# A two-layer decoder step on Trainium2: VectorE's weight sums tied behind a job's third sum, two PSUM products moved ahead of a square, and the norm's eps moved ahead of a low part

## The chip, the core and the metric

The kernel runs on one core of one Trainium2 chip. The metric is the device time of one execution in microseconds (us), the median of three runs; lower is better. The engines are named as in the profile: PE is TensorE (PEld its weight loads), DVE is VectorE, ACT is ScalarE, POOL is GpSimd, SP is SyncE, whose queue issues most loads.

## The reference, cut to what matters

```python
def rmsnorm(x, g):
    y = xf * lax.rsqrt(jnp.mean(xf * xf, axis=-1, keepdims=True) + RMS_EPS)
    return (y * g).astype(x.dtype)

def swiglu(x, w_gate, w_up, w_down):
    return (jax.nn.silu(x @ w_gate) * (x @ w_up)) @ w_down

def short_conv_mixer(x, buf, w_in, w_conv, w_out):
    b, c, h = jnp.split(x @ w_in, 3, axis=-1)
    u = c * h
    full = jnp.concatenate([buf, u], axis=1)
    y = sum(w_conv[j] * full[:, j:j + L] for j in range(CONV_WIDTH))
    return (b * y) @ w_out, full[:, -(CONV_WIDTH - 1):]

def trunk(...):                          # layer 0: short convolution, layer 1: retention
    for i in range(DEPTH):
        h = rmsnorm(x, norm_mix[i])
        m, st = short_conv_mixer(h, ...) if i % 2 == 0 else retention_mixer(h, ...)
        x = x + m
        x = x + swiglu(rmsnorm(x, norm_ffn[i]), ffn_w_gate[i], ffn_w_up[i], ffn_w_down[i])
    return rmsnorm(x, final_norm), ...
```

The model width is 1024, the FFN's hidden width 2816; 512 prompt tokens and 32 sample tokens are handled together, so a token axis has 544 columns, in two halves of 272 (`HT`). All is float32.

## The kernel before, in words

**Precision.** A float32 product is made of three faster matmuls: each operand is split into a high part (`h`, `wh`, a copy on ACT) and a low part (`l`, `wl`, the difference, on DVE), and high·high, high·low and low·high are summed in PSUM. `split` makes both parts; `mixed` makes the low part's first half on DVE and its second half with an accumulating DMA that POOL issues.

**Jobs.** Most projections are done two 128-row output tiles at a time, as a 2×2 block product in seven instead of eight products (`Job`). `weights7` loads the two weight tiles on SP's queue into three rotating buffers (`w`), and makes four sums of them on DVE (lines 357 to 360 before the change: `s1 = a21 + a22`, `s2 = s1 - a11`, `a21 = a11 - a21`, `w4 = a12 - s2`) and then the parts p1 (products 1 and 2), p2 (6 and 5), p3 (7 and 4) and p4 (3), which are named `wh/wl`, `h2/l2`, `wh/wl` and `h4/l4`. One product is 12 matmuls of 272 columns (line 411). Each product's PSUM result is handed on at once: `u1`, `u2`, `p5` and the last one, `c21`, are copied by ACT, while `c11`, `c12` and `u3` are added by DVE (line 516). The accumulator of products 1, 6, 7, 4 is one PSUM bank: product 4 may not write it before DVE has read it for `u3`, the sum behind product 7. `run` prepares the weights of job i+1 when job i begins.

**Order.** The instructions are recorded in the order of the code, and a scheduler that works with estimated costs then sets the order on each engine; each engine works its queue off in that order. `tc.issue_after(x)` keeps the instructions in its block behind `x` where both are on one engine.

**The convolution.** `start` makes the first output tile of b, c and h directly from x as it arrives, `products` the second one; the norm's scale `R` comes only later, so the results are multiplied by `R` (b) or `R2 = R·R` (c) behind the products (lines 674 to 677). Then come eight jobs (h and b of tiles 2 and 3; c, h and b of tiles 4, 5 and of 6, 7).

**The norms in front of the FFN.** `rms_scale` is a generator whose steps are woven between the matmuls of the first two FFN jobs: five matmuls with the mean's column (line 274), eps on DVE (line 249) and the power on POOL (line 252), some empty steps (`rest`), and five matmuls that spread the result over the partitions (line 256), which ACT copies into `R` (lines 285 and 286). `paced(steps, 4)` leaves out the first four places.

Of the kernel before, what the change touches and what calls it, by code (L numbers as in the profile page):

```python
# [52 lines left out]
def hybrid_decode_kernel(ctx: ExitStack, tc: tile.TileContext, a: dict, o: dict):  # L53
    nc = tc.nc
# [143 lines left out]
    def halves(t):  # L198
        return t.rearrange("p (a b) -> p a b", a=2)
# [57 lines left out]

    def rms_scale(sample=False, pt=None, rest=4):

# [6 lines left out]
        for tt in range(n):  # L266
# [8 lines left out]
            if tt < n - 1:  # L275
                yield
        rsqrt(rN[:, :n], ms[:, :n], n)
        for _ in range(rest):
            yield
# [57 lines left out]

    def weights7(src1, src2, sw, n, adding=False, spare=None, first=1, fourth=False, whole=False, later=()):

# [14 lines left out]
        with ExitStack() as behind:  # L354
            for made in later:
                behind.enter_context(tc.issue_after(made.ins))
            nc.vector.tensor_add(s1, a21, a22)
            nc.vector.tensor_sub(s2, s1, a11)
            nc.vector.tensor_sub(a21, a11, a21)
            nc.vector.tensor_sub(w4, a12, s2)  # L360

        behind, p1, p2 = last_minus[0], parts2(2 * n), parts2(2 * n, sw, ("h2", "l2"))
        if whole:
            split(*p1, w1)
        else:
            (split_adding if adding else mixed)(*p1, w1, src1)
        with tc.issue_after(behind.ins) if adding else ExitStack():
            split(*p2, w2)
        p3 = parts2(2 * n)
        with ExitStack() as after:  # L370
            for made in later:
                after.enter_context(tc.issue_after(made.ins))
            mixed(*p3, w3, src2)
        p4 = parts2(n, sw, ("h4", "l4"))
        with tc.issue_after(behind.ins) if adding else ExitStack():
            split(*p4, w4)

# [109 lines left out]

    def run(jobs, order, after, steps, ahead=False):

        jobs[0].order = order  # L490
        jobs[0].begin()
        jobs[0].weave = jobs[1].weave = steps
        for i, job in enumerate(jobs):
            nxt = jobs[i + 1] if i + 1 < len(jobs) else None
            if nxt is not None:
                nxt.prepare()
            apart = i == 0 and (ahead or not order)
            job.middle(nxt if apart else None)
            if nxt is not None and not (i == 0 and ahead):
                nxt.begin()  # L500
            job.end()
            after(i)

    last_add = [None]

    def summed(dst, finish):


        def take(what, src):
# [3 lines left out]
            if what in first:  # L513
                nc.scalar.activation(first[what], src, AF.Copy)
            elif what in more:
                last_add[0] = nc.vector.tensor_add(more[what], more[what], src)  # L516
            finish(what, src)

# [4 lines left out]
    with ExitStack() as c0:  # L523
# [148 lines left out]
        pts.append(products(1, range(3), steps))  # L672
        signal(0)
        nc.vector.tensor_mul(R2, R, R)
        for d, r, j in ((c, R2, 1), (b, R, 0)):
            nc.vector.tensor_mul(halves(d[:, 0, :]), halves(d[:, 0, :]), r)
            each(lambda p, di, ri: nc.vector.tensor_mul(di, p, ri), pts[1][j], halves(d[:, 1, :]), r)
        for i in range(2):
# [55 lines left out]
        mixed_in(b, taps(0), 0)  # L734
        run(jobs, (2, 5, 6), lambda i: None, iter(()), True)

# [18 lines left out]
    def ffn(layer, next_gain, then=None):  # L755
        with ExitStack() as c1:
# [194 lines left out]
            if layer == 1:  # L951
                jobs[0].places["later"] = [residuals[5]]
            jobs[0].prepare(layer == 1)
            made_in = MADE if layer == 0 else list(range(KT))
# [16 lines left out]

            steps = paced(rms_scale(rest=7), 4)
            run(jobs, (), after, steps)
# [929 lines left out]
```

## Time and profile before

| | |
|---|---|
| median of three runs | 1387.44 us (1385.43 to 1388.99) |
| the profiled execution's own time | 1386.94 us |
| its span | 1385.2 us |
| PE, PEld, DVE, ACT, POOL busy | 99%, 95%, 82%, 59%, 16% |
| HBM | 158 GB/s read and written over the span |

The span is the stretch from the first to the last instruction of the program; 1.7 us of the profiled execution lie around it. PE is busy nearly all the time, so the first question for each edit is whether PE waits at that place. A PE that waits for a semaphore for a short time is hardly seen in busy shares: it is seen in the distance between the starts of neighbouring matmuls.

### The profile page before, as it was taken

The page shows a single profiled execution, that of the slowest core. Times are in us where ns is not written, and L with a number is a line of the kernel's source. Part 1 is how long each engine was busy: PE and PEld are TensorE (multiplying, and loading weights), DVE is VectorE, ACT ScalarE, POOL GpSimd, SP SyncE. Part 2 cuts the span into 40 slices and gives each one's busy share as a digit, 9 for nine tenths or more (in the row PEclk, how much of TensorE's full clock was granted, in tenths as well). Part 3 has the DMA queues.
Part 4 walks back from the last instruction along what each step waited for, and adds up shares of the span by engine and source line. Part 5 has one row for each costly group of instructions (what it writes and reads, how often), then busy time and mean ns, then how long its engine had stood idle before and what let it go on. Part 6 is the DMA issues. An engine that isn't in the chain of part 4 may idle for free.

```text
span 1385.2 us, 26505 instructions
## 1 busy us (share of the span) xinstructions
PE 1375.7 (99%) x10420; PEld 1313.7 (95%) x10420; DVE 1134.0 (82%) x1929; ACT 822.9 (59%) x1288; POOL 217.8 (16%) x249
## 2 busy tenths in 40 slices
PE   9999999999999999999999999999999999999998
PEld 9999999999999999999978887887899999999997
DVE  6988889898989888777868586586799898989875
ACT  7666567667667656767641413224377767667654
POOL 0111011212222213211200000000112212221212
PEclk9999999999999999999999999999999999999999
DMA  6477347777777754777666455475756777777752
GB/s 224 115 162 169 109 107 162 176 169 179 151 184 154 165 126 123 201 175 221 187 230 228 149 186 201 136 261 183 220 131 157 171 176 173 155 178 166 165 111 88
DMA packets 99438, 232.89 MB, mean 168 GB/s; under 512 B 9809, under 2 KB 33889, under 8 KB 98929
## 3 DMA queue, kind: packets, MB, share of 16 engines
q1 hardware_dynamic: 68464, 167.26, 39.2%
q0 software_dynamic: 28400, 55.82, 23.4%
q10 hardware_dynamic: 2448, 8.12, 1.5%
q8 instruction: 81, 1.33, 0.4%
q14 instruction: 45, 0.36, 0.1%
HBM read 191.05 MB, written 28.42 MB: 158 GB/s over the span
## 4 chain that ended last, share of the span: by engine, by line
PE 94%; DVE 3%; ACT 1%; DMA 1%; issue 0%; POOL 0%; DVEq 0%; SPq 0%; POOLq 0%; ACTq 0%
PE sm L411 43%; PE mm L411 16%; PE mm L187 14%; PE sm L187 5%; PE sm L1344 2%; PE sm L1345 2%; PE sm L1346 2%; PE sm L175 2%; PE sm L176 1%; PE sm L177 1%; PE sm L1594 1%; DVE ol L203 1%; DMA w<-in_cvin_dram 1%; PE mm L1355 1%; PE mm L1612 1%; PE mm L1522 1%
## 5 line engine op out<-in xcount | busy, mean ns | idle before, releaser
L411 PE MATMUL sm<-oh,wh 128*128 128x272 f32 x856 | 247.2, 289 | 1.3 <-DVE h L516 1.3
L411 PE MATMUL sm<-ol,wh 128*128 128x272 f32 x856 | 246.2, 288 | 0.0
L411 PE MATMUL sm<-oh,wl 128*128 128x272 f32 x856 | 246.1, 288 | 0.0
L202 ACT ACTIVATE h<-w 128x512 fp32r<-128x512 f32 (+3 forms) x171 | 137.7, 805 | 85.8 <-PE mm L411 77.6
L203 DVE TENSOR_TENSOR l<-w,h 128x512 fp32r<-128x512 f32 (+3 forms) x171 | 154.6, 905 | 23.2 <-ACT h L202 21.0
L333 ACT ACTIVATE wh<-w 128x1024 fp32r<-128x1024 f32 (+1 forms) x133 | 132.9, 999 | 53.5 <-PE sm L411 43.4
L411 PEld LDWEIGHTS sm<-oh,wh 128*128 128x128 f32 x856 | 161.3, 188 | 1.9 <-DVE h L516 1.5
L411 PEld LDWEIGHTS sm<-oh,wl 128*128 128x128 f32 x856 | 161.0, 188 | 0.0
L411 PEld LDWEIGHTS sm<-ol,wh 128*128 128x128 f32 x856 | 160.8, 188 | 0.0
L202 ACT ACTIVATE wh<-w 128x1024 fp32r<-128x1024 f32 (+3 forms) x80 | 69.2, 874 | 123.7 <-PE mm L187 61.2
L411 PE MATMUL sm<-parts,wh 128*128 128x272 f32 x736 | 142.6, 288 | 0.0
L336 POOL DMA_DIRECT2D wl<-in_ffgu_dram x87 | 81.7, 939 | 320.5 <-ACT wl L335 136.0
L411 PEld LDWEIGHTS sm<-parts,wh 128*128 128x128 f32 x736 | 115.5, 188 | 0.0
L411 PE MATMUL mm<-oh,h 128*128 128x272 f32 x396 | 114.0, 288 | 0.0
L411 PE MATMUL mm<-oh,l 128*128 128x272 f32 x396 | 113.4, 286 | 0.0
L411 PE MATMUL mm<-ol,h 128*128 128x272 f32 x396 | 113.1, 286 | 0.0
L411 PE MATMUL sm<-parts,wl 128*128 128x272 f32 x368 | 106.3, 289 | 0.0
L335 ACT ACTIVATE wl<-wh 128x512 fp32r<-128x512 f32 (+1 forms) x172 | 102.4, 595 | 2.2
L334 DVE TENSOR_TENSOR wl<-w,wh 128x512 fp32r<-128x512 f32 (+1 forms) x133 | 86.3, 649 | 16.3 <-ACT wh L333 16.2
L203 DVE TENSOR_TENSOR wl<-w,wh 128x1024 fp32r<-128x1024 f32 (+3 forms) x80 | 81.2, 1023 | 14.0 <-ACT wh L202 13.4
L187 PE MATMUL mm<-parts,wh 128*128 128x272 f32 x488 | 82.6, 291 | 0.1
L411 PE MATMUL sm<-oh,h 128*128 128x272 f32 x284 | 82.4, 290 | 0.0
(384 smaller groups left out, 3822.4 us busy)
## 6 DMA issues: line engine op xcount, KB each, us to landing
w<-in_ffgu_dram SPq DMA_DIRECT2D x66, 512.0 KB
wl<-in_ffgu_dram POOLq DMA_DIRECT2D x87, 256.0 KB, 5.7
S<-in_rets_dram SPq DMA_DIRECT2D x16, 1024.0 KB
out_rets_dram<-S SPq DMA_DIRECT2D x16, 1024.0 KB
w<-in_ffdn_dram SPq DMA_DIRECT2D x36, 384.0 KB
cb<-in_ffgu_dram SPq DMA_DIRECT2D x22, 512.0 KB
w<-in_cvin_dram SPq DMA_DIRECT2D x21, 512.0 KB
wl<-in_ffdn_dram POOLq DMA_DIRECT2D x48, 192.0 KB, 4.8
```

The source lines that it names most:

```text
L175: nc.tensor.matmul(out, lh, rh, start=start, stop=False, skip_group_check=True)
L187: last_product[0] = nc.tensor.matmul(half(pt, hf)[:, :HT], w[:, c], act[k][:, hf * HT : (hf + 1) * HT], start=(first and k == ks[0] and i ...
L202: h = nc.scalar.activation(dh, src, AF.Copy)
L203: last_low[0] = nc.vector.tensor_sub(dl, src, dh.bitcast(F32))
L333: nc.scalar.activation(wh, w, AF.Copy)
L334: last_mixed[0] = nc.vector.tensor_sub(wl[:, :n], w[:, :n], wh[:, :n].bitcast(F32))
L335: nc.scalar.activation(wl[:, n:], wh[:, n:].bitcast(F32), AF.Copy, scale=-1.0)
L336: nc.gpsimd.dma_start(wl[:, n:], src[:, 1, :] if len(src.shape) == 3 else src[:, n:], accum_op=ALU.add)
L411: last = nc.tensor.matmul(out, w[:, c], b, start=(first and j == 0 and i == 0), stop=(j == len(self.ks) - 1 and i == 2), skip_group_check= ...
L1344: nc.tensor.matmul(out, xh[kt][:, ts_], wh[:, cw], start=(kt == 0), stop=False)
L1345: nc.tensor.matmul(out, xh[kt][:, ts_], wl[:, cw], start=False, stop=False)
L1346: last = nc.tensor.matmul(out, xl[kt][:, ts_], wh[:, cw], start=False, stop=(kt == KT - 1))
```

## The change: what it does

There are three edits.

1. In the convolution's `run` each job from the third on gets a `guard`: the DVE instructions that make its weights' sums, and the low parts p1 and p3 that DVE makes of them, are kept behind the `u3` sum of the job two before it.
2. Behind `products(1, ...)` the two PSUM products for b (`pts[1][0]` times `R`) stand ahead of `R2 = R·R` and the two products in SBUF; the one for c stays behind them.
3. In both FFNs `rms_scale` starts one place later (`paced(..., 5)`) with one empty step less (`rest=6`), and the split of p4 of the second job is held back until eps has been recorded (`held`, `then`).

```diff
-    def rms_scale(sample=False, pt=None, rest=4):
+    def rms_scale(sample=False, pt=None, rest=4, then=()):
...
         rsqrt(rN[:, :n], ms[:, :n], n)
+        for made in then:
+            made()
         for _ in range(rest):
             yield
...
-    def weights7(src1, src2, sw, n, adding=False, spare=None, first=1, fourth=False, whole=False, later=()):
+    def weights7(src1, src2, sw, n, adding=False, spare=None, first=1, fourth=False, whole=False, later=(), held=None, guard=()):
...
-            for made in later:
+            for made in (*guard, *later):
                 behind.enter_context(tc.issue_after(made.ins))
             nc.vector.tensor_add(s1, a21, a22)
...
-        if whole:
-            split(*p1, w1)
-        else:
-            (split_adding if adding else mixed)(*p1, w1, src1)
+        with ExitStack() as held_back:
+            for made in guard:
+                held_back.enter_context(tc.issue_after(made.ins))
+            if whole:
+                split(*p1, w1)
+            else:
+                (split_adding if adding else mixed)(*p1, w1, src1)
...
-            for made in later:
+            for made in (*guard, *later):
                 after.enter_context(tc.issue_after(made.ins))
             mixed(*p3, w3, src2)
         p4 = parts2(n, sw, ("h4", "l4"))
-        with tc.issue_after(behind.ins) if adding else ExitStack():
-            split(*p4, w4)
+        if held is not None:
+            held.append(lambda: split(*p4, w4))
+        else:
+            with tc.issue_after(behind.ins) if adding else ExitStack():
+                split(*p4, w4)
...
-    def run(jobs, order, after, steps, ahead=False):
+    def run(jobs, order, after, steps, ahead=False, guard=False):
+        last_third[0] = None
...
             if nxt is not None:
+                if guard and last_third[0] is not None:
+                    nxt.places["guard"] = [last_third[0]]
                 nxt.prepare()
...
                 last_add[0] = nc.vector.tensor_add(more[what], more[what], src)
+                if what == "u3":
+                    last_third[0] = last_add[0]
...
+        each(lambda p, di, ri: nc.vector.tensor_mul(di, p, ri), pts[1][0], halves(b[:, 1, :]), R)
         nc.vector.tensor_mul(R2, R, R)
-        for d, r, j in ((c, R2, 1), (b, R, 0)):
-            nc.vector.tensor_mul(halves(d[:, 0, :]), halves(d[:, 0, :]), r)
-            each(lambda p, di, ri: nc.vector.tensor_mul(di, p, ri), pts[1][j], halves(d[:, 1, :]), r)
+        nc.vector.tensor_mul(halves(c[:, 0, :]), halves(c[:, 0, :]), R2)
+        nc.vector.tensor_mul(halves(b[:, 0, :]), halves(b[:, 0, :]), R)
+        each(lambda p, di, ri: nc.vector.tensor_mul(di, p, ri), pts[1][1], halves(c[:, 1, :]), R2)
...
-        run(jobs, (2, 5, 6), lambda i: None, iter(()), True)
+        run(jobs, (2, 5, 6), lambda i: None, iter(()), True, True)
...
+            fourth = []
+            jobs[1].places["held"] = fourth
             jobs[0].prepare(layer == 1)
...
-            steps = paced(rms_scale(rest=7), 4)
+            steps = paced(rms_scale(rest=6, then=fourth), 5)
```

How the queues move. On SP's and POOL's queues no row changes its place. On VectorE the largest move is in the convolution's first two jobs. In these rows `w_86`, `w_87` are the weights of the third job and `w2_88`, `wl_90`, `wl_94` what is made of them; `h_68<-...sm_67` is the first job's `u3`, `h_68<-...mm_82` its `c12`, `b_84<-...sm_85` the second job's `c11`; `l4_80` belongs to the second job. Before:

```order
L357 TENSOR_TENSOR w2_88_915<-w_86_913 128x512
L358 TENSOR_TENSOR w2_88_915<-w2_88_915,w_87_914 128x512
L516 TENSOR_TENSOR b_84_855<-b_84_855,sm_85_857 128x272
L359 TENSOR_TENSOR w_86_913<-w_87_914,w_86_913 128x512
L516 TENSOR_TENSOR h_68_769<-h_68_769,sm_67_756 128x272
L360 TENSOR_TENSOR cb_67<-w_87_914,w2_88_915 128x512
L516 TENSOR_TENSOR h_68_769<-h_68_769,mm_82_815 128x272
L203 TENSOR_TENSOR l4_80_798<-w4_72_774,h4_79_797 128x512
L334 TENSOR_TENSOR wl_90_923<-w_87_914,wh_89_922 128x512
L334 TENSOR_TENSOR wl_94_933<-w_86_913,wh_93_932 128x512
L707 TENSOR_TENSOR u_104<-c_36_557,h_68_769 128x2x512
L708 TENSOR_TENSOR u_104<-c_36_557,h_68_769 128x2x8x4
```

With the change (lines count from the new file):

```order
L527 TENSOR_TENSOR b_84_855<-b_84_855,sm_85_857 128x272
L527 TENSOR_TENSOR h_68_769<-h_68_769,sm_67_756 128x272
L359 TENSOR_TENSOR w2_88_915<-w_86_913 128x512
L527 TENSOR_TENSOR h_68_769<-h_68_769,mm_82_815 128x272
L203 TENSOR_TENSOR l4_80_798<-w4_72_774,h4_79_797 128x512
L360 TENSOR_TENSOR w2_88_915<-w2_88_915,w_87_914 128x512
L361 TENSOR_TENSOR w_86_913<-w_87_914,w_86_913 128x512
L721 TENSOR_TENSOR u_104<-c_36_557,h_68_769 128x2x512
L362 TENSOR_TENSOR cb_67<-w_87_914,w2_88_915 128x512
L722 TENSOR_TENSOR u_104<-c_36_557,h_68_769 128x2x8x4
L336 TENSOR_TENSOR wl_90_923<-w_87_914,wh_89_922 128x512
L336 TENSOR_TENSOR wl_94_933<-w_86_913,wh_93_932 128x512
```

The `u3` sum now stands ahead of all sums of the third job's weights, and the low parts `wl_90` and `wl_94` now stand behind the products u = c·h. Further down in the convolution no VectorE row moves by more than two places.

On VectorE in front of the first layer's FFN, `rN<-mm_268` is eps, `l4_263` the low part p4 of the second job, and `g_252` its first job's sums. Before:

```order
L516 TENSOR_TENSOR g_252_2385<-g_252_2385,sm_265_2430 128x272
L516 TENSOR_TENSOR g_252_2385<-g_252_2385,sm_251_2372 128x272
L203 TENSOR_TENSOR l4_263_2413<-w4_255_2389,h4_262_2412 128x512
L249 TENSOR_SCALAR rN_86<-mm_268_2475 128x5
L516 TENSOR_TENSOR g_252_2385<-g_252_2385,sm_264_2416 128x272
```

With the change:

```order
L527 TENSOR_TENSOR g_252_2385<-g_252_2385,sm_265_2428 128x272
L527 TENSOR_TENSOR g_252_2385<-g_252_2385,sm_251_2372 128x272
L249 TENSOR_SCALAR rN_86<-mm_268_2476 128x5
L203 TENSOR_TENSOR l4_263_2413<-w4_255_2389,h4_262_2412 128x512
L527 TENSOR_TENSOR g_252_2385<-g_252_2385,sm_264_2414 128x272
```

Eps and the low part change places; on PE there the first mean matmul stands three matmuls later.

On ScalarE in the second layer's FFN, `u_1526<-sm_1525` is the second job's `u2` (its accumulator behind product 6), `wh_1532`, `h2_1534`, `wh_1536` are the third job's high parts, `g_1511<-g_1511` is the gate's silu. Before:

```order
L514 ACTIVATE u_1526_11972<-sm_1525_11951 128x272
L333 ACTIVATE wh_1532_12041<-w_1529_12032 128x1024
L285 ACTIVATE R_85<-mm_1527_11977 128x384
L286 ACTIVATE R_85<-mm_1527_11977 128x160
L871 ACTIVATE g_1511_11887<-sm_1510_11874 128x272
L335 ACTIVATE wl_1533_12042<-wh_1532_12041 128x512
L202 ACTIVATE h2_1534_12043<-w2_1530_12033 128x1024
L333 ACTIVATE wh_1536_12051<-w_1528_12031 128x1024
L873 ACTIVATE g_1511_11887<-g_1511_11887 128x1088
```

With the change:

```order
L335 ACTIVATE wh_1532_12041<-w_1529_12032 128x1024
L287 ACTIVATE R_85<-mm_1527_11978 128x384
L288 ACTIVATE R_85<-mm_1527_11978 128x160
L885 ACTIVATE g_1511_11887<-sm_1510_11874 128x272
L337 ACTIVATE wl_1533_12042<-wh_1532_12041 128x512
L202 ACTIVATE h2_1534_12043<-w2_1530_12033 128x1024
L887 ACTIVATE g_1511_11887<-g_1511_11887 128x1088
L335 ACTIVATE wh_1536_12051<-w_1528_12031 128x1024
L525 ACTIVATE u_1526_11970<-sm_1525_11949 128x272
```

The copy `u2` has gone from the head of this stretch to its end, and the silu ahead of `wh_1536`. In step with it, PE now does 15 matmuls of the third job (12 of `sm_1542`, 3 of `mm_1555`) ahead of the second job's product 7 (`sm_1525<-wh_1519`), four matmuls of the second job stand behind the first job's product 4 and the spread, and on VectorE `wl_1533` stands behind the gate's first product with `R` (L872) instead of ahead of it.

More of the change, by code (lines that the diff above doesn't have):

```diff
@@ L502, in run @@
             after(i)
-    last_add = [None]
+    last_add, last_third = [None], [None]
     def summed(dst, finish):
```

## The prediction

> **What bounds the kernel now.** I read the page first, then the waits of PE, then the chain that ended last, and then the timeline around every place that the change touches.
>
> ```profile
> span 1385.2 us, 26505 instructions
> PE 1375.7 (99%) x10420; PEld 1313.7 (95%) x10420; DVE 1134.0 (82%) x1929; ACT 822.9 (59%) x1288; POOL 217.8 (16%) x249
> ```
>
> ```profile
> PE sm L411 <- DVE h L516: 1.3, 1, 1.3
> ```
>
> ```profile
> 93.83 4.51 PE sm L411 x36
> ```
>
> PE works through the whole span, so the time changes only by what PE waits. The chain's row gives the measure: 36 matmuls in 4.51 us, one every 0.125 us. A larger distance between two starts is a wait. The longest listed wait is on VectorE's `h` sum of line 516, and the timeline shows it:
>
> ```profile
> 67.89 0.29 PE L411 MATMUL mm<-parts,l 128*128 128x272 f32 x1
> 69.47 0.39 PE L411 MATMUL sm<-oh,wh 128*128 128x272 f32 x1 [1.30 <-DVE h L516]
> 69.70 0.29 PE L411 MATMUL sm<-ol,wh 128*128 128x272 f32 x1
> ```
>
> ```profile
> 65.06 0.69 DVE L357 TENSOR_TENSOR w<-w 128x512 f32<-128x512 f32 x1
> 67.43 0.69 DVE L358 TENSOR_TENSOR w<-w,w 128x512 f32<-128x512 f32 x1 [1.68 <-DMA w<-in_cvin_dram]
> 68.04 0.43 DVE L516 TENSOR_TENSOR b<-b,sm 128x272 f32<-128x272 f32 x1
> ...
> 68.99 0.43 DVE L516 TENSOR_TENSOR h<-h,sm 128x272 f32<-128x272 f32 x1
> ```
>
> PE was due at 67.89 + 0.125 = 68.02 and starts at 69.47, and the next one comes 0.23 after it instead of 0.125: 1.45 + 0.11 = 1.56 us lost. VectorE was idle meanwhile: its queue stood at line 358 for a load, with the `u3` sum that PE needed behind it.
>
> **Edit 1, the guard.** `u3` now stands ahead of the third job's sums. Product 7 had ended by about 67.4 (the six matmuls up to 67.89 come behind it: 67.89 - 5 x 0.125 = 67.26 for the first of them), so `u3` can run from about 67.5 to 67.9, and PE is let in when it is due. That takes away the whole 1.56. But VectorE's sums, which ran in part during the old wait, now begin only at 67.8, and what they make is needed later:
>
> ```profile
> 72.25 0.69 DVE L334 TENSOR_TENSOR wl<-w,wh 128x512 fp32r<-128x512 f32 x1 [0.68 <-ACT wh L333]
> 72.86 1.22 DVE L707 TENSOR_TENSOR u<-c,h 128x1024 f32<-128x1024 f32 x1
> ...
> 75.30 1.23 DVE L203 TENSOR_TENSOR l<-w,h 128x1024 fp32r<-128x1024 f32 x1 [0.96 <-ACT h L202]
> ...
> 85.55 0.68 DVE L334 TENSOR_TENSOR wl<-w,wh 128x512 fp32r<-128x512 f32 x1
> ```
>
> ```profile
> 80.00:90.00 10.00, 10.00 (x82) 10.00 (x81) 9.90 (x18) 8.11 (x13) 2.60 (x3) 1.00 0.41 87
> ```
>
> ```profile
> 86.10 0.41 PE L411 MATMUL sm<-parts,wh 128*128 128x272 f32 x2
> 86.35 0.33 PE L411 MATMUL sm<-parts,wl 128*128 128x272 f32 x1
> ```
>
> From 75.30 VectorE does not rest (9.90 of 10 us between 80 and 90), and the low part that it ends at 85.55 + 0.68 = 86.23 is read by PE at 86.35, in the first matmul that it can be. PE cannot be earlier there than VectorE. So I count VectorE's chain in the new order, with 0.6 from one 512-column instruction to the next (67.43 to 68.04) and 0.4 for a 272-column one: `u3` at 67.47, the first weight sum at 67.85, `c12` at 68.45, then the second job's low part `l4`. That one waits for ScalarE:
>
> ```profile
> 69.07 0.61 ACT L202 ACTIVATE h<-w 128x512 fp32r<-128x512 f32 x1
> ```
>
> It starts at 69.07 + 0.61 + 0.05 = 69.73. Line 358's sum follows at 70.33, 359's at 70.93, u at 71.53, 360's at 72.75 (behind 1.22), the small product at 73.35, the two low parts at 73.5 and 74.1, and the row of 75.30 at 74.7 to 74.8 (ScalarE's high part for it, which stands behind u, ends about then). This is 0.55 earlier than before; the same unbroken work follows, so the low part of 85.55 comes 0.55 earlier. Edit 1: -0.55; the other 1.0 of the 1.56 is paid back as a new wait at that matmul. Bounds: 0 (one more late copy of ScalarE in the chain uses it up) and -1.56. VectorE's late low parts also hold the weights' buffers longer:
>
> ```profile
> 62.09 11.21 SPq L351 DMA_DIRECT2D w<-in_cvin_dram  x4
> ```
>
> The fourth of these loads ends its issue at 73.30, right behind the low part of 72.25; it and the third move some 2 us. A load takes 5.3 (62.09 to line 358's release at 67.43), so the one that was freed at about 71.6 and now is at 74.1 lands at 79.4; its sum stands five instructions, some 3 us, ahead of that low part, at about 82. SP's and POOL's rows keep their order. I cost this at nothing, with these 2 to 3 us as its cover; if the cover goes, the convolution's gain goes with it.
>
> **Edit 2, b's products ahead of R².**
>
> ```profile
> 37.05 0.41 PE L187 MATMUL mm<-parts,wl 128*128 128x272 f32 x2
> 37.48 0.65 PE L187 MATMUL sm<-parts,wh 128*128 128x272 f32 x2
> ```
>
> ```profile
> 36.90 0.78 DVE L677 TENSOR_TENSOR b<-sm,R 128x272 f32<-128x272 f32 x2
> ```
>
> ```profile
> 34.00:62.00 28.00, 27.82 (x50) 1.00 0.38 85
> ```
>
> ```profile
> DVE wl L334 <- ACT wh L333: 0.2, 1, 0.2
> ```
>
> ```profile
> 62.11 0.39 PE L411 MATMUL sm<-parts,wl 128*128 128x272 f32 x1
> ```
>
> PE was due at 37.30, starts at 37.48 as VectorE leaves the first bank, and its next two take 0.65 instead of 0.41: 0.42 us. With the two products three SBUF operations earlier that wait goes. But VectorE is busy 27.82 of the 28 us that follow, and at 62.11 PE again waits for it (0.39 instead of 0.29, and a start late by 0.07). The same work in another order ends at the same time there, but for the one wait of 0.2 on ScalarE, whose copy waits for a buffer that PE leaves. So of 0.42 only 0.2 is left at 62, and the load and the copies behind it move along. Edit 2: -0.2, between 0 and -0.42.
>
> The Trainium skill, Perfetto Trace Analysis, "Identifying the Most-Contended Engine", says to improve the engine with the highest occupancy and to judge TensorE by its weight loads. By that rule, stage by stage, VectorE (27.82 of 28.00) is the one here, and moving its work without lessening it gives nothing: 0 instead of -0.2, and 0 instead of -0.55 at edit 1. The row with 1.68 idle speaks against the rule for edit 1, the full window for it in edit 2.
>
> **Edit 3, first layer.**
>
> ```profile
> 197.85 0.29 PE L411 MATMUL sm<-oh,wl 128*128 128x272 f32 x1
> 198.28 0.35 PE L274 MATMUL mm<-cb,sqacc 128*128 128x1 f32 x2
> ...
> 204.48 0.29 PE L411 MATMUL sm<-oh,wl 128*128 128x272 f32 x1
> 204.94 0.32 PE L256 MATMUL mm<-cb,rN 128*128 128x128 f32 x1 [0.18 <-POOL rN L252]
> ```
>
> ```profile
> 202.84 0.69 DVE L203 TENSOR_TENSOR l<-w,h 128x512 fp32r<-128x512 f32 x1 [1.07 <-ACT h L202]
> 203.45 0.16 DVE L249 TENSOR_SCALAR rN<-mm 128x5 f32<-128x5 f32 x1
> ```
>
> ```profile
> 203.69 1.20 POOL L252 TENSOR_TENSOR rN<-rN,expo 128x5 f32<-128x5 f32 x1 [2.04 <-DVE rN L249]
> ```
>
> The first mean matmul starts 0.31 after it was due (197.97), because the squares' sum is not ready. Three matmuls, 0.375 us, now come ahead of it: the 0.31 goes. The spread starts 0.34 after it was due (204.60), behind POOL's power, which waits for eps, which stands behind a low part that waits 1.07 for ScalarE. With eps ahead of that it runs about 1.2 earlier and POOL ends at about 203.6: the 0.34 goes too. The low part moves back by 0.16 and is read by PE far later. Together -0.65; below this nothing, above it 0 if a later buffer gives it back, but the list of PE's waits has none behind it in this FFN, so I keep it.
>
> **Edit 3, second layer.**
>
> ```profile
> 1030.51 0.29 PE L411 MATMUL sm<-ol,wh 128*128 128x272 f32 x1
> 1030.95 0.35 PE L274 MATMUL mm<-cb,sqacc 128*128 128x1 f32 x2 [0.15 <-DVE sqacc L236]
> ...
> 1041.14 0.29 PE L411 MATMUL sm<-oh,wh 128*128 128x272 f32 x1
> ```
>
> ```profile
> 1040.34 1.07 ACT L202 ACTIVATE h<-w 128x1024 fp32r<-128x1024 f32 x1
> 1041.29 1.07 ACT L333 ACTIVATE wh<-w 128x1024 fp32r<-128x1024 f32 x1
> 1042.24 1.12 ACT L873 ACTIVATE g<-g 128x1088 f32<-128x1088 f32 x1
> ```
>
> ```profile
> 1039.98 1.29 DVE L872 TENSOR_TENSOR g<-g,R 128x1088 f32<-128x1088 f32 x1
> ```
>
> Here the first mean matmul moves by one matmul only: 0.12 of its 0.31 goes. The spread did not wait. But the queues moved more. The second job's product 7 (1041.14) now stands behind 15 more matmuls, 1.88 us, so it is due at 1041.14 + 1.88 - 0.12 = 1042.9. Ahead of it ScalarE must have made the copy `u2`, now behind h2, silu and `wh` in its queue. These end 0.2 to 0.7 earlier than before, as the spread is four matmuls earlier; with 1.0 each, h2 from 1039.65 to 1040.1, `wh` done by 1042.6 to 1043.0, and 0.4 for the copy: 1043.0 to 1043.4. PE waits 0.1 to 0.5, and 0.1 more for its restart. I take 0.3. Net +0.2, between -0.12 and +1.0 (below).
>
> **The sum.** -0.55 - 0.2 - 0.65 + 0.2 = -1.2. Against the profiled execution (1386.94) that is 1385.7; the median of the three runs lies 0.5 above it, so the forecast is 1387.44 - 1.2 = 1386.2.
>
> **Rivals.** *All waits go and stay away*: VectorE's chain is shorter than I count, or low parts are needed later. Then 0.42 + 1.56 + 0.65 + 0.12 = 2.75 less: 1384.7. Against it: the busy windows and the match of 86.23 with 86.35. *VectorE's stage decides, as by the rule above*: the convolution gives nothing, the FFNs -0.65 + 0.2: 1387.0. For it: 27.82 of 28.00; against it the 1.68 and 0.96 of idle time in between. *Slower: VectorE's queue only passes the delay on.* The convolution gives nothing, and in the second layer the low part `wl` that used to be ready ahead of the product with R comes behind it, at 1039.98 + 1.29 + 0.68 = 1041.95, where PE, due with it at 1041.14 + 0.25 - 0.12 = 1041.27, waits 0.7; the copy then costs 0.3 and a restart 0.1, +1.1 - 0.12; with the first layer's -0.65 it is +0.3: 1387.7. It decides if R does not come earlier, so that the product with R keeps its 1039.98. That the guard does nothing is out: VectorE's rows move.
>
> **How the numbers follow.** Forecast 0.45, all stays away 0.15, stage decides 0.2, slower 0.2. The single runs spread from 2.0 below to 1.6 above their median, a median of three by perhaps half of that; from 1384.7 and 1387.7 with this the range is 1384.0 to 1388.7. A bound of 0.3%, about what a measurement of this kernel can tell from no change, is 4.2 us, more than any sum here: faster 0.04, the same 0.92, slower 0.04, the outer ones for a load that I costed at nothing.
>
> **What would show it.** In the new profile PE's wait for line 516's `h` sum is gone; the matmul that reads the low part of 85.55 waits about 1 us; the rows at 198 and 205 follow at 0.125; around 1043 product 7 waits for ScalarE's `u`. I am wrong if PE passes the matmul at 86 without a wait, if loads in the convolution are waited for longer, or if PE waits anywhere behind 206 in the first FFN.

## The result, and the profile after

| | before | changed |
|---|---|---|
| median | 1387.53 us (22 runs, 1385.43 to 1390.57) | 1385.18 us (22 runs, 1384.16 to 1387.38) |
| profiled execution, span | 1385.2 us | 1383.4 us |

The ratio is 0.9982, with a 95% interval of 0.9976 to 0.9988: the change took away 2.35 us (1.7 to 3.3). The forecast was 1.2.

The page of the changed kernel, its first part, and the waits of PE (us in total, times, longest):

```profile
span 1383.4 us, 26506 instructions
PE 1374.6 (99%) x10420; PEld 1313.2 (95%) x10420; DVE 1133.7 (82%) x1929; ACT 822.7 (59%) x1288; POOL 218.1 (16%) x249
```

```profile
PE sm L419 <- DVE b L527: 0.7, 1, 0.7
PE mm L187 <- DVE parts L222: 0.3, 1, 0.3
PE sm L419 <- ACT b L525: 0.2, 1, 0.2
```

The wait of 1.3 us for VectorE's `h` sum is gone. Two waits are new: one for VectorE's `b` sum (line 527 is the old 516) and one for a copy of ScalarE (525, the old 514). The timeline of PE in the changed kernel shows where they are; start and duration stand first, and brackets hold idle time and what ended it:

```profile
67.73 0.29 PE L419 MATMUL mm<-parts,l 128*128 128x272 f32 x1
67.86 0.33 PE L419 MATMUL sm<-oh,wh 128*128 128x272 f32 x1
...
72.29 0.28 PE L419 MATMUL mm<-oh,l 128*128 128x272 f32 x1
72.78 0.39 PE L419 MATMUL sm<-oh,wh 128*128 128x272 f32 x1 [0.21 <-ACT b L525]
...
85.16 0.41 PE L419 MATMUL mm<-parts,h 128*128 128x272 f32 x2
85.51 0.39 PE L419 MATMUL sm<-parts,wl 128*128 128x272 f32 x1
...
109.02 0.28 PE L419 MATMUL mm<-parts,l 128*128 128x272 f32 x1
110.01 0.39 PE L419 MATMUL sm<-oh,wh 128*128 128x272 f32 x1 [0.70 <-DVE b L527]
```

At 67.86 product 4 of the first job starts when it is due, 0.13 after its neighbour. At 72.78 product 7 of the second job starts 0.49 after the matmul ahead of it instead of 0.125. At 85.51, the place of the forecast's large wait, 0.1 is lost and another 0.1 in its restart, and at 110.01, with 0.99 from start to start, 0.86.

**A ledger of PE's starts.** PE issues 10,420 matmuls in every kernel here. The start of the n-th one, less that of the n-th one in the profile of before, is how far PE is ahead; the step of this number across a place is what the place gives (minus) or takes. The table has these steps in us for each profiled execution, named by the place's time in before. FFN 1 and FFN 2 are the FFNs of the first and the second layer. The second-to-last column is a stage in which no instruction moved (the retention, 900 to 925). The last column is the whole from 13.5 us on; ahead of that the loads of the start scatter by up to 0.7. Beside the columns, small steps at 61 to 63, 118, 300 and 580 to 650 go into it.

| profiled execution | 37.5 | 69.5 | 74 | 86 | 110 | FFN 1 | FFN 2 | 900-925 | all |
|---|---|---|---|---|---|---|---|---|---|
| changed | -0.42 | -1.52 | +0.48 | +0.15 | +0.88 | -0.76 | -0.07 | -0.60 | -2.00 |
| a2_after (changed, again) | -0.42 | -1.53 | +0.45 | +0.15 | +0.73 | -0.74 | -0.05 | -0.60 | -2.04 |
| e1_guard | -0.24 | -1.52 | +1.02 | +0.15 | +1.05 | 0 | 0 | -0.60 | +0.26 |
| e2_bsums | -0.42 | -0.68 | 0 | 0 | +0.13 | 0 | 0 | -0.61 | -1.72 |
| e4_eps0 | -0.37 | +0.20 | 0 | 0 | +0.76 | -0.76 | 0 | -0.60 | -0.54 |
| e5_no_eps1 | -0.42 | -1.52 | +1.06 | +0.15 | +0.26 | -0.75 | 0 | -0.31 | -1.57 |
| e6_no_guard | -0.42 | -0.65 | 0 | 0 | +1.42 | -0.78 | -0.04 | +0.44 | +0.14 |
| f2_sums_first | -0.42 | -1.52 | 0 | +0.16 | +0.24 | -0.76 | -0.04 | -0.56 | -2.90 |
| f3_pool_low | -0.42 | -1.52 | +1.54 | +0.16 | -0.08 | -0.74 | -0.05 | 0 | -1.00 |
| f4_both | -0.42 | -1.52 | 0 | +0.15 | 0 | -0.75 | -0.07 | -0.60 | -3.18 |
| f4_again | -0.42 | -1.52 | 0 | +0.15 | -0.08 | -0.77 | -0.05 | -0.39 | -3.26 |
| g1_both_no_eps1 | -0.42 | -1.53 | 0 | +0.15 | -0.06 | -0.78 | 0 | +0.46 | -1.94 |
| g2_both_no_bsums | -0.32 | -1.52 | 0 | +0.23 | -0.08 | -0.77 | -0.06 | -0.60 | -3.18 |

It reads in two ways. Down a column, a step that stands in all kernels with an edit and in none without it is the edit's: 69.5 (-1.52 with the guard, between -0.68 and +0.20 without it), 74, both FFNs. A step that comes and goes in kernels with the same code there is scatter of one execution: 110, and 900 to 925, where the profile of before was 0.6 slower than most.

### The profile page after: what moved, and what is told of

It reads as the page before. It is cut to its first block, busy times and chain, and to the rows that moved or that the text cites. A ratio compares the mean times of both kernels' runs of the same rounds, so it can differ in the third digit from the quotient of the medians.

```text
span 1383.4 us, 26506 instructions
## 1 busy us (share of the span) xinstructions
PE 1374.6 (99%) x10420; PEld 1313.2 (95%) x10420; DVE 1133.7 (82%) x1929; ACT 822.7 (59%) x1288; POOL 218.1 (16%) x249
## 4 chain that ended last, share of the span: by engine, by line
PE 95%; DVE 2%; DMA 1%; ACT 1%; issue 0%; POOL 0%; SPq 0%; DVEq 0%; ACTq 0%; POOLq 0%
PE sm L419 43%; PE mm L419 16%; PE mm L187 15%; PE sm L187 5%; PE sm L1360 2%; PE sm L1362 2%; PE sm L1361 2%; PE sm L175 2%; PE sm L176 1%; PE sm L177 1%; PE sm L1610 1%; DMA w<-in_cvin_dram 1%; DMA x<-in_xT_dram 1%; PE mm L1371 1%; PE mm L1628 1%; PE mm L1538 1%
```

## The experiments: one edit at a time

Each diff is against the changed kernel, and each ratio against the kernel before on the same chip. Medians of different chips are compared here only where the text says so: the kernel before has 1386.93 us beside e1 to e5, 1386.69 beside e6 and f2 to f4_both, and 1387.47 beside the last four.

**e1_guard**: edit 1 alone.

```diff
-        each(lambda p, di, ri: nc.vector.tensor_mul(di, p, ri), pts[1][0], halves(b[:, 1, :]), R)
         nc.vector.tensor_mul(R2, R, R)
...
-            jobs[1].places["held"] = fourth
-            steps = paced(rms_scale(rest=6, then=fourth), 5)
+            steps = paced(rms_scale(rest=7), 4)
```

> Edit 1 alone: the third job's weight sums wait for u3; b's products and the norms stand as before. The prediction's theory (VectorE's unbroken queue hands 1.0 of the 1.56 us back at the matmul that reads the low part of 85.55): -0.55 us, PE waits about 1 us near 86 and runs free behind it. Rival A, read from the changed kernel's trace (the gain is handed back at 110, behind a weight load that lands 0.17 earlier though it was issued 0.88 earlier, because the DMA engines are full from 84 to 102): -1.0 to -1.3 at 69 to 86, and -0.4 to 0 behind 110. Rival B (the wait is gone for good): -1.5, kept to the end.

Measured: 1386.48 us against 1386.93; ratio 0.9997 (0.9988 to 1.0005). The wait at 69 goes whole, but 1.02 of it is back at 74, 0.15 at 86 and 1.05 at 110. So the forecast's place (86) is wrong, rival B is wrong, and rival A misses 74.

**e2_bsums**: edit 2 alone.

```diff
-        run(jobs, (2, 5, 6), lambda i: None, iter(()), True, True)
+        run(jobs, (2, 5, 6), lambda i: None, iter(()), True)
...
-            jobs[1].places["held"] = fourth
-            steps = paced(rms_scale(rest=6, then=fourth), 5)
+            steps = paced(rms_scale(rest=7), 4)
```

> Edit 2 alone: b's products with R ahead of R's square. Prediction: the 0.42 us wait at 37.48 goes, 0.2 of it comes back at 62, so -0.2. Rival A (nothing comes back at 62, the whole train behind it, loads and all, moves with PE): -0.42 at every place from 38 to 120. Rival B (the loads at 85 to 102 hold as in the changed kernel): -0.42 to 110, then about -0.2 to 0.

Measured: 1386.29 us; ratio 1.0003 (0.9994 to 1.0012), which is inconclusive on so small a term. In the trace -0.42 at 37.5 and nothing back at 62, as by rival A up to there. At 69.5 PE waited 0.68 less than in the profile of before although the guard isn't there: that wait scatters with the load.

**e4_eps0**: edit 3 in the first layer alone.

```diff
-        each(lambda p, di, ri: nc.vector.tensor_mul(di, p, ri), pts[1][0], halves(b[:, 1, :]), R)
         nc.vector.tensor_mul(R2, R, R)
...
-        run(jobs, (2, 5, 6), lambda i: None, iter(()), True, True)
+        run(jobs, (2, 5, 6), lambda i: None, iter(()), True)
...
-            jobs[1].places["held"] = fourth
+            if layer == 0:
+                jobs[1].places["held"] = fourth
-            steps = paced(rms_scale(rest=6, then=fourth), 5)
+            steps = paced(rms_scale(rest=6, then=fourth), 5) if layer == 0 else paced(rms_scale(rest=7), 4)
```

> Edit 3 in the first layer's FFN alone. Prediction: -0.65 us, 0.31 at the first mean matmul and 0.34 at the spread, and nothing given back up to the FFN's end. Rival (a later buffer gives it back): 0. Beyond 300 us the code is unchanged: what the starts of PE's matmuls lose or win there against the kernel before is scatter of one execution.

Measured: 1386.47 us; ratio 1.0000 (0.9991 to 1.0008). In the trace the FFN gives 0.36 at the mean matmul and 0.40 at the spread, and keeps it to its end; the convolution, whose code is that of before, lost 0.76 at 110 in this execution. The clock can't tell 0.7 us here; the ledger can.

**e5_no_eps1**: the changed kernel with edit 3 undone in the second layer.

```diff
-            jobs[1].places["held"] = fourth
+            if layer == 0:
+                jobs[1].places["held"] = fourth
-            steps = paced(rms_scale(rest=6, then=fourth), 5)
+            steps = paced(rms_scale(rest=6, then=fourth), 5) if layer == 0 else paced(rms_scale(rest=7), 4)
```

> The changed kernel without edit 3 in the second layer's FFN. Prediction (edit 3 costs 0.2 there): 0.2 us below the changed kernel, and PE's waits at 1030.95 and 1044.21 as before. By the changed kernel's trace (its waits of 0.18, 0.14 and 0.16 us there take the place of 0.31, 0.08 and 0.17): the same within 0.1. Whatever the second layer does, the stages ahead of it should read as in the changed kernel: -0.4 behind the convolution and -0.7 in the first FFN.

Measured: 1385.11 us; ratio 0.9989 (0.9980 to 0.9997). It is level with the changed kernel's 1385.18 and 1385.37, but these come from other chips, and its ratio is the higher one (the changed kernel's are 0.9982 and 0.9983): so the clock does not show the 0.2 us of the forecast, nor their opposite. The stages ahead of it read as in the changed kernel but for the scatter at 74 and 110. On the same chip e5 lies 1.37 below e1, which has the guard alone: edits 2 and 3 (first layer), 1.2 in the ledger, show in the clock too.

**e6_no_guard**: the changed kernel with edit 1 undone.

```diff
-        run(jobs, (2, 5, 6), lambda i: None, iter(()), True, True)
+        run(jobs, (2, 5, 6), lambda i: None, iter(()), True)
```

> The changed kernel without edit 1 (edits 2 and 3 stay). Theory now: the guard takes away a wait of 0.9 to 1.8 us at 69 and gives back 0.5 to 1.1 us at 74, where ScalarE's copy of the second job's u2 stands behind a high part that waits for VectorE's moved sums, and 0.15 at 86; so this kernel is 0.2 to 0.6 us above the changed one, with PE's wait at 69 back and none at 74. Rival A (the prediction's -0.55 by VectorE's queue): 0.55 above, and a wait of 1 us at 86 in the changed kernel, none here. Rival B (edit 1 nets nothing): the same as the changed kernel. The wait at 110 is expected anywhere between 0 and 1 us in any of these kernels.

Measured: 1386.64 us; ratio 0.9996 (0.9988 to 1.0005), 1.3 to 1.5 above the changed kernel's medians of other chips. The waits change places as foretold: back at 69, none at 74, none at 86. By the clock the difference is more than foretold, but in the ledger the guard's own places make only 0.24 of the 2.14 between the two totals (0.87 - 0.48 - 0.15); 0.54 stands at 110, 1.04 at 900 to 925 and 0.26 at 580 to 650, where executions of the same code differ as much.

## The experiments: where the guard's gain goes

Why does PE wait at 74? VectorE and ScalarE of the changed kernel:

```profile
69.46 0.69 DVE L203 TENSOR_TENSOR l<-w,h 128x512 fp32r<-128x512 f32 x1 [0.77 <-ACT h L202]
70.07 0.69 DVE L360 TENSOR_TENSOR w<-w,w 128x512 f32<-128x512 f32 x1
70.67 0.68 DVE L361 TENSOR_TENSOR w<-w,w 128x512 f32<-128x512 f32 x1
```

```profile
67.18 1.06 ACT L335 ACTIVATE wh<-w 128x1024 fp32r<-128x1024 f32 x1 [1.47 <-DMA w<-in_cvin_dram]
68.27 0.63 ACT L337 ACTIVATE wl<-wh 128x512 fp32r<-128x512 f32 x1
68.81 0.62 ACT L202 ACTIVATE h<-w 128x512 fp32r<-128x512 f32 x1
69.61 0.40 ACT L715 ACTIVATE h<-sm 128x272 f32<-128x272 f32 x1 [0.18 <-PE sm L419]
71.39 1.06 ACT L335 ACTIVATE wh<-w 128x1024 fp32r<-128x1024 f32 x1 [1.38 <-DVE w L361]
72.36 0.37 ACT L525 ACTIVATE b<-sm 128x272 f32<-128x272 f32 x1
```

The second job's low part `l4` waits 0.77 for ScalarE. Behind it stand the sums that the guard has moved (360 and 361). ScalarE's high part `wh` of p3 waits 1.38 for the sum 361, and behind that `wh`, in ScalarE's queue, stands the copy `u2` that lets PE write product 7. At 72.36 + 0.37 it is done, and PE starts at 72.78.

The first of ScalarE's rows shows what sets the size of this wait: ScalarE is released by a weight load of the third job. It is the load of SP's row 62.09, which ended VectorE's wait at 67.43 in before. In the five executions with the guard and this order (changed, a2, e1, e5, f3) that row starts between 67.18 and 68.50, and PE starts at 74 5.60 or 5.61 behind it in each. In the four without the guard (before, e2, e4, e6) PE starts at 69.5 2.04 or 2.05 behind VectorE's row that this load releases. So the waits at 69.5 and at 74 scatter with one and the same load: the guard takes PE from behind VectorE, but in this order the load still reaches PE, by way of ScalarE, at the next place.

**f2_sums_first**: the changed kernel with the split that makes `l4` recorded behind the third job's sums. Only the order changes.

```diff
             nc.vector.tensor_sub(w4, a12, s2)
+        for made in then:
+            made()
...
                     nxt.places["guard"] = [last_third[0]]
+                if guard and i < 2:
+                    nxt.places[("held", "then")[i]] = fourths
```

> The changed kernel with the second job's low part l4 behind the third job's weight sums on VectorE, so that these don't wait with it for ScalarE and ScalarE's high part p3 and the u2 copy behind it come some 1.5 us earlier. Theory (the give-back at 74 comes through ScalarE's queue): PE's wait at 74 of 0.5 to 1.1 us is gone, all 1.5 of the guard is kept to 85; 0.5 to 0.8 us below the changed kernel if the load near 100 doesn't hold it. Rival (VectorE's unbroken queue sets the low part read at 86): the wait moves from 74 to 86, no gain. Rival (the weight load that lands at 100 holds all): the gain is there to 105 and given back at 110.

Measured: 1384.65 us; ratio 0.9984 (0.9975 to 0.9993). Its ScalarE and PE:

```profile
70.14 1.06 ACT L335 ACTIVATE wh<-w 128x1024 fp32r<-128x1024 f32 x1
71.33 0.40 ACT L530 ACTIVATE b<-sm 128x272 f32<-128x272 f32 x1
```

```profile
72.49 0.29 PE L421 MATMUL mm<-oh,l 128*128 128x272 f32 x1
72.62 0.29 PE L421 MATMUL sm<-oh,wh 128*128 128x272 f32 x1
```

The high part no longer waits, the copy is ready 0.9 ahead of need, and PE passes at 0.13. In all five executions with this order the step at 74 is 0, also in g2, where the load releases ScalarE last of all (68.58); in all five with the guard and the old order it is 0.45 to 1.54. The wait did not move to 86, where the step stays at 0.15 to 0.23: VectorE's sums no longer stand behind `l4`, and its low part comes earlier too (85.19 instead of 85.45). So the give-back at 74 goes through ScalarE's queue: shown by the trace. The clock does not show f2's gain by itself: its ratio is that of the changed kernel (0.9984 beside 0.9982), and the 0.5 below the changed median is a comparison of two chips.

Why does PE wait at 110? The `b` sum there stands in VectorE's queue behind a chain that begins with a wait for a weight load. The load's row on SP's queue in before, then VectorE in before, in the changed kernel, and the changed kernel's window of that time (busy per engine, then granted clock, DMA share, GB/s):

```profile
94.11 0.33 SPq L351 DMA_DIRECT2D w<-in_cvin_dram  x1
```

```profile
100.37 0.69 DVE L358 TENSOR_TENSOR w<-w,w 128x512 f32<-128x512 f32 x1 [2.38 <-DMA w<-in_cvin_dram]
```

```profile
100.20 0.69 DVE L360 TENSOR_TENSOR w<-w,w 128x512 f32<-128x512 f32 x1 [3.27 <-DMA w<-in_cvin_dram]
```

```profile
90.00:100.00 10.00, 10.00 (x82) 10.00 (x81) 6.31 (x10) 5.93 (x10) 1.73 (x2) 1.00 1.03 242
```

PE is 1.03 ahead of before from 86 to 110, and the load's issue 0.88 (93.23), but VectorE is released only 0.17 earlier. The DMA engines are busy through this stretch (share 1.03). Beside the load an accumulating DMA of 544 KB runs, the low part `yl` of the convolution's result. In every execution that waits here PE starts 9.80 or 9.81 behind VectorE's release, so the load decides. These two profiles suggest that the gain won ahead of the load ends at it. The other profiles do not bear that out. From its issue to VectorE's release the load takes 6.3 to 7.7 us in the nine executions with the transfer, and the step at 110 goes with that length and not with PE's lead: e4, 0.1 ahead, loses 0.76 behind a load of 7.0, and f2, 1.8 ahead, loses 0.24 behind one of 6.3. Before, with 6.3, is the shortest of the nine; the mean step is 0.58 in the four without the guard and 0.63 in the five with it.

**f3_pool_low**: the changed kernel with that low part made by GpSimd in SBUF.

```diff
-            (split if f == KT - 2 else split_adding)(yhh, yll[:, f : f + 2, :], b)
+            if f == 2:
+                nc.scalar.activation(yhh, b, AF.Copy)
+                nc.gpsimd.tensor_tensor(yll[:, f : f + 2, :], b, yhh.bitcast(F32), op=ALU.subtract)
+            else:
+                (split if f == KT - 2 else split_adding)(yhh, yll[:, f : f + 2, :], b)
```

> The changed kernel, but the low part of the second yh pair is computed by GpSimd in SBUF instead of ScalarE's negation and an accumulating DMA of 544 KB, which runs from 88 to 97 beside the weight load that VectorE waits for until 100. Theory (the wait at 110, 0.1 to 1.05 us in the six executions, comes from that load, slowed by DMA engines that are full from 86 to 102): the load takes 5.3 to 6 us instead of 6.3 to 7.1, and PE's wait at 110 is under 0.15; 0.4 to 0.9 us below the changed kernel. Rival (the chain of VectorE behind the load sets it, the load lands as late): no change at 110.

Measured: 1384.98 us; ratio 0.9987 (0.9978 to 0.9995). At 110 the step is -0.08: PE doesn't wait. The median is 0.2 to 0.4 below the changed kernel's of other chips, less than the 0.4 to 0.9 expected, and its ratio isn't lower; the profiled execution lost 1.54 at 74, the most of all.

**f4_both**: f2 and f3 together; the diff is theirs.

> Both: the low part l4 behind the sums, and the 544 KB transfer left to GpSimd. If both causes are right the convolution keeps the guard's 1.5 us and b's 0.2 to 0.4 us to 118 and beyond: 1 to 1.6 us below the changed kernel, 3 below the kernel before. If the gains only run into the next load, as much as the better of the two alone.

Measured: 1384.19 us (1383.35 to 1385.05); ratio 0.9979 (0.9971 to 0.9988). That is 2.5 below the kernel before on its chip, where 3 was expected. In the ledger the convolution keeps 1.8 us. Then four kernels side by side on one chip, the changed one among them.

**a2_after**: the changed kernel again, no edit. **f4_again**: f4_both again.

> The changed kernel once more, beside the version with both further edits (l4 behind the sums, the second low part left to GpSimd). By the places of the traces so far it should read -0.42 at 38, -1.52 at 70, +0.5 to +1.5 at 74, +0.15 at 86, 0 to +1 at 110, -0.76 in the first FFN and -0.04 in the second; about 1385.2 us. If the waits at 74 and 110 were not its own but one execution's, one of them is missing here.

> The version with both further edits, beside the changed kernel on the same chip: without the waits at 74 and 110, which cost the changed kernel 1.2 us together on the mean of its looks, it is 0.7 to 1.5 us below it and its times spread less. Rival (the traces' waits at 74 and 110 are paid elsewhere in the undisturbed runs): no difference.

Measured: 1385.37 us (0.9983, 0.9975 to 0.9992) and 1383.82 us (0.9975, 0.9966 to 0.9985). The nine runs of f4_again lie between 1383.46 and 1384.66, the eleven of a2_after between 1384.27 and 1387.67; the medians differ by 1.55, at the upper end of the 0.7 to 1.5 expected. The two intervals against before overlap, so this rests on the runs side by side and on the waits. Of f4_again, the load on SP's queue, VectorE behind it, the window, and PE:

```profile
93.81 2.38 SPq L353 DMA_DIRECT2D w<-in_cvin_dram  x2
```

```profile
97.84 0.69 DVE L360 TENSOR_TENSOR w<-w,w 128x512 f32<-128x512 f32 x1 [1.06 <-DMA w<-in_cvin_dram]
```

```profile
90.00:100.00 10.00, 10.00 (x82) 10.00 (x81) 8.94 (x16) 5.69 (x10) 1.73 (x2) 1.00 0.78 176
```

```profile
108.07 0.28 PE L421 MATMUL mm<-parts,l 128*128 128x272 f32 x1
108.19 0.29 PE L421 MATMUL sm<-oh,wh 128*128 128x272 f32 x1
```

From its issue to VectorE's release the load takes 4.0 us (93.81 to 97.84) instead of 6.3 in before (94.11 to 100.37) and 7.0 in the changed kernel (93.23, the start of its SP row, to 100.20), at a DMA share of 0.78 instead of 1.03; PE passes 110 (here 108.19) at 0.12. In five of five executions without the 544 KB transfer the load takes 3.6 to 4.5 us and the step at 110 is 0 or below; in nine with it, before among them, the step lies between 0 and 1.42. That taking the transfer out shortens the load and ends the wait: shown. The edit also shifts the smaller transfers beside it on GpSimd's queue (in f4_again to 88.58 and 90.89, in the changed kernel at 87.07 and 91.87), so how much is due to the 544 KB alone isn't shown. Nor is what makes the load vary among the nine.

**g1_both_no_eps1**: f4_both with edit 3 undone in the second layer (the diff of e5). **g2_both_no_bsums**: f4_both with edit 2 undone:

```diff
-        each(lambda p, di, ri: nc.vector.tensor_mul(di, p, ri), pts[1][0], halves(b[:, 1, :]), R)
         nc.vector.tensor_mul(R2, R, R)
-        nc.vector.tensor_mul(halves(c[:, 0, :]), halves(c[:, 0, :]), R2)
-        nc.vector.tensor_mul(halves(b[:, 0, :]), halves(b[:, 0, :]), R)
-        each(lambda p, di, ri: nc.vector.tensor_mul(di, p, ri), pts[1][1], halves(c[:, 1, :]), R2)
+        for d, r, j in ((c, R2, 1), (b, R, 0)):
+            nc.vector.tensor_mul(halves(d[:, 0, :]), halves(d[:, 0, :]), r)
+            each(lambda p, di, ri: nc.vector.tensor_mul(di, p, ri), pts[1][j], halves(d[:, 1, :]), r)
```

> The version with both further edits, without edit 3 in the second layer's FFN. The prediction has that edit cost 0.2 us: then this is 0.2 below the version with it. By the traces it nets -0.04 (0.33 gained at the first mean matmul, 0.22 to 0.26 and 0.12 given back later): the same within 0.2.

> The version with both further edits, with R's square ahead of b's products as before (edit 2 undone). The prediction has edit 2 give 0.2, half of it lost at 62; the looks at kernels without it had a wait of 0, 0.18 and 0.05 less than the first look's 0.42 at 37.5, and none of the gain came back at 62: PE waits 0.05 to 0.42 us at 37.5 here and the time is 0.05 to 0.4 above the version with edit 2.

Measured: 1384.67 us (0.9979, 0.9970 to 0.9988) and 1384.59 us (0.9976, 0.9966 to 0.9985). Both lie above f4_again, by 0.85 and 0.77, more than the 0.2 and the 0.05 to 0.4 expected. So no run shows edit 3 in the second layer to cost time. But its gain stays open: e5 shows none, the ledger shows 0.04 to 0.07, and g1's own profiled execution lost its time in places without an edit (0.42 at 300, 0.46 at 900 to 925). Edit 2's difference is of the foretold sign; its trace has 0.10 at 37.5 and 0.08 at 86 of the 0.77.

## Why the prediction was right, and where not, step by step

**The whole.** Faster, and by less than can be told by one median: right. The forecast's size was half of the measured one; 1385.18 lies inside the range, whose ends are 0.2 to 0.3 off their own rule (half of 2.0 below 1384.7 and half of 1.6 above 1387.7 give 1383.7 and 1388.5). In the ledger the places that the prediction named give, with the changed kernel's first row, -0.42 - 1.52 + 0.48 + 0.15 + 0.88 - 0.76 - 0.07 = -1.26, and -1.41 in its second, beside the forecast's -1.2. That these agree is luck: edit 1 came to -0.89 in that row, or to -0.01 with the load at 110, instead of -0.55, edit 2 to -0.42 instead of -0.2, and edit 3 to -0.83 instead of -0.45. Of the rest of the -2.00, 0.6 is the retention of the one profile of before. What makes the many runs differ by 2.35 rather than 1.3 isn't settled: only one execution of each kernel has a trace, and the scattering places (69.5 without the guard, 110, 900 to 925) are as large as the difference.

**Edit 1, that the wait goes:** right, 1.52 of 1.56. **That 1.0 of it comes back at the matmul that reads the low part of 85.55:** wrong in place and size. The step that failed is "VectorE's chain in the new order": its times were right (sums at 70.33 and 70.93, found at 70.07 and 70.67), but only VectorE's own readers on PE were looked for. The sum 359 is read by ScalarE, and the copy behind that was late by 74: 0.48 came back there. At 86 it was 0.15. VectorE does let PE in there, as foretold: this row ends at 85.45, and PE starts at 85.51.

```profile
84.77 0.68 DVE L336 TENSOR_TENSOR wl<-w,wh 128x512 fp32r<-128x512 f32 x1
```

But the reader now stands behind two more matmuls (those of 85.16), 0.25 us that the forecast, which kept PE's old order, did not have. Net -0.89 up to there instead of -0.55, and nearly nothing behind 110 in the first profile; without the guard the four profiles (before, e2, e4, e6) come to 0, -0.55, +0.96 and +0.77 from 69.5 to 110, with it and without the further edits (changed, a2, e1, e5) to -0.01, -0.20, +0.70 and -0.05, a mean of 0.30 against 0.11. So in the ledger the guard gives 0.2 in the mean of four and four, less than it scatters.

**The loads, costed at nothing:** wrong for the changed kernel's profile, and named beforehand as what would speak against the forecast: VectorE waits 3.27 instead of 2.38 near 100. The looked-for cover was the sum's place near 82, not the load near 100. But the wait there is not the guard's: the load is as long in kernels without it (7.0 in e4, 7.7 in e6), and the mean step at 110 is the same with and without. What the forecast could not see is that the load in the profile of before was the shortest of nine; the mean step at 110 in the other eight is 0.68.

**Edit 2, -0.2:** right in size for another reason. The give-back at 62 that halved it did not come: in the changed kernel PE is ahead by the same 0.42 there, and the wait at 62 stays what it was. Of the ten executions with edit 2 only f3 gave more than 0.05 back at 62: 0.26, after it had won 0.16 from 38 to 60.

```profile
61.63 0.41 PE L419 MATMUL sm<-parts,wh 128*128 128x272 f32 x2
61.95 0.40 PE L419 MATMUL sm<-parts,wl 128*128 128x272 f32 x1
```

The full VectorE window did not hold PE: what ends last at 62 moved with it. The Trainium skill, Perfetto Trace Analysis, "Identifying the Most-Contended Engine", says to optimize the engine with the highest occupancy first. The prediction's rival drew from it that a new order alone gives nothing where VectorE is full; here it gave 0.42 us. But the old wait was smaller on the mean than its one profile: 0.42, 0.18, 0.05 and 0.10 in the four executions with the old order (0.42 less the steps of e1, e4 and g2), 0.19.

**Edit 3, first layer, -0.65:** right, -0.74 to -0.78 in all eleven executions with it. PE, VectorE and GpSimd of the changed kernel:

```profile
198.06 0.29 PE L419 MATMUL sm<-oh,wl 128*128 128x272 f32 x1
198.18 0.30 PE L274 MATMUL mm<-cb,sqacc 128*128 128x1 f32 x2
...
203.94 0.29 PE L419 MATMUL sm<-oh,wl 128*128 128x272 f32 x1
204.06 0.71 PE L256 MATMUL mm<-cb,rN 128*128 128x128 f32 x5
```

```profile
201.53 0.15 DVE L249 TENSOR_SCALAR rN<-mm 128x5 f32<-128x5 f32 x1
202.31 0.69 DVE L203 TENSOR_TENSOR l<-w,h 128x512 fp32r<-128x512 f32 x1 [0.62 <-ACT h L202]
```

```profile
201.77 1.20 POOL L252 TENSOR_TENSOR rN<-rN,expo 128x5 f32<-128x5 f32 x1 [0.28 <-PE sm L419]
```

Both rows follow at 0.12; eps stands ahead of the low part, and the power ends at 202.97, a whole us before the spread.

**Edit 3, second layer, +0.2:** wrong sign. Product 7 does wait for `u2`, as foretold:

```profile
1041.14 0.28 PE L419 MATMUL mm<-oh,l 128*128 128x272 f32 x1
1041.32 0.39 PE L419 MATMUL sm<-oh,wh 128*128 128x272 f32 x1
```

But it is late by 0.05 (due at 1041.27) and loses 0.1 for its restart, not 0.3; the first mean matmul's wait falls from 0.31 to 0.18, as foretold; and an old wait of 0.17 (in before at 1044.21, for ScalarE's copy at 1043.76) is gone. The step counted the new wait and not the old one. The wait of the slower rival, for the low part `wl` behind the product with `R`, is there too, but small: `wl` ends at 1039.48, PE starts at 1039.54, and 0.14 is lost instead of 0.7 and a restart, because `R` comes earlier (the product with it starts at 1037.59 instead of 1039.98).

**The rivals.** All waits gone and staying away (-2.75) is the nearest in time, but not what happened: a wait came back through ScalarE, and another stands behind the load at 110. VectorE's stage decides: refuted by edit 2, whose 0.42 stays, and by f2 and f4_both; but its zero for edit 1 was near. Slower: refuted.

## What to carry to other kernels

When an instruction is moved behind another on one engine, follow each of its readers into that reader's own queue, and look at what stands behind it there: the wait came back through a third engine's copy. Where a load ends a wait, ask also which instruction the load holds next once the wait is gone: here it was the same load at 69.5 and at 74. A wait in one profile is one draw: before costing its removal, look at whether what ends it (a load, a full queue) can vary.

## What was not expected of the hardware

In f4_again GpSimd's subtraction holds VectorE up. GpSimd's row and two of VectorE's:

```profile
85.38 3.26 POOL L678 TENSOR_TENSOR yl<-b,yh 128x1088 fp32r<-128x1088 f32 x1 [4.33 <-ACT yh L677]
```

```profile
86.84 2.34 DVE L359 TENSOR_TENSOR w<-w 128x512 f32<-128x512 f32 x1
...
90.06 0.68 DVE L360 TENSOR_TENSOR w<-w,w 128x512 f32<-128x512 f32 x1
```

A 512-column sum of two SBUF operands takes 0.68 us, and here, beside GpSimd's subtraction, 2.34; it ends at 89.18, 0.54 after GpSimd's 88.64. In the other four executions with this subtraction it takes 2.33 to 2.35. The Trainium skill, SBUF — State Buffer, "Terms", says that the two share one pair of ports and that the loser waits for the other's whole instruction; this row agrees. It is not so for every row: a low part of two SBUF operands that starts at 85.54, 0.16 after GpSimd's row, takes its usual 0.68. The hold-up cost PE nothing here, as VectorE waited for a load behind it anyway (1.06 left).
